# Emission by rank, lazily given operand buffers and one-buffer builders in a streaming encoder step

## Chip, core and metric

The kernel runs on one core of a Trainium2 chip. The metric is device time in microseconds of one execution; a kernel's time is the median of its runs.

## The reference, cut to what matters

Two layers run over 1024 prompt tokens and 32 sample tokens, 1056 in all. A layer normalises, projects, mixes with latent attention and retention, projects back and adds; then comes the part that the change touches:

```python
def channel_and_ple(h, p_i, norm_ffn_w, w_ff1, w_ff2, norm_ple_w, w_ple_gate, w_ple_proj):
    u = rms_norm(h, norm_ffn_w) @ w_ff1
    h = h + jnp.square(jax.nn.relu(u)) @ w_ff2
    gate = jax.nn.sigmoid(rms_norm(h, norm_ple_w) @ w_ple_gate)
    return h + (p_i @ w_ple_proj) * gate
```

The model width is 1024, the feed-forward width 4096, the depth 2.

## The kernel before

Activations stand with features on partitions and the 1056 tokens along the free dimension. `h` (8 x 1056, f32) stays in SBUF for the whole run. Every f32 factor of a product is split into two f16 halves, `hi` by ACT (a copy) and `lo` by DVE or POOL (the f32 value less `hi`), and a product is three f16 matmuls.

**The feed-forward products** use a two by two block scheme with seven products in place of eight. A weight unit `W[n]` has seven combined weights, each split; an operand has seven forms too, numbered 0 to 6, and product i of 1 to 7 takes the form `PROD[i]`: 1 takes 0, 7 takes 5, 6 takes 4, 4 takes 2, 5 takes 3, 2 takes 1 and 3 takes 6, in this order of work. `PROD` and the token groups are constants: three thirds `PG` of 2 x 176 tokens and two halves `PW` of 2 x 264. There are 32 weight units in a layer: four rounds `e` with four units of ff1 and then four of ff2. The first two units of ff1 go third by third, both side by side; all later ones go in halves. A product on one half is a block of twelve matmuls (four operand tiles, three matmuls each).

**Entry.** The output projection runs third by third (lines 1787 to 1806). `norm_chain` (L631) follows it: squares on ACT, their sums on PE, a power on POOL, a diagonal on ACT, its broadcast on PE (`acc,ones` in PE's order), then four times `four` (L717), which multiplies two tiles of `h` (DVE), makes four sums and differences, and splits the seven forms into the operand `x2`. `four` held one arena buffer `R` and one temporary `R3`.

**ff1 and ff2.** `ff1_units` (L943) runs the seven products of its units; product partial sums are read out of PSUM after each product and go on being added to in the same bank (`A` collects 1, 6, 5 and 3). `ff1_chains` (L870) evacuates (`ra`, `rb`), applies the squared relu and builds the seven forms of the ff2 operand `rr`; the pair of forms (4, 5) was split by one instruction on both (`r<-ra,r`, 2 x 264). `ff2_units` (L965) multiplies `rr` and adds into `h`.

**Buffers.** `arena` has 29 large SBUF buffers, `temps` 12 smaller ones, `weights` 14, `stages` 2 for incoming weights; PSUM has eight banks of four kinds (`mm`, `mx`, `st`, `o`). `operands` (L768) took all buffers of two operands at once, and the caller waited until seven were free.

**What sets the order.** The program text is not the order. `Pipe` (L300) holds generators in a heap and `Model` keeps an estimated time for each engine. A chain yields an operation, `_step` emits it when the model says that its inputs and its engine are ready; PE's instructions are written by the main thread, which polls the heap between blocks. `Either` (L202) picks between DVE and POOL for a two-input operation: before, by the earlier start with a bias of 0.2 us for the first named. What is emitted first stands first in its engine's queue, and every queue runs in order. `load_group` (L801) combines the weights of a unit with four subtractions and splits seven weights, `load` (L1027) starts it.

## Time and profile before

| | |
|---|---|
| runs (3) | 2709.64, 2712.25, 2714.51 us; median 2712.25 |
| the profiled execution | 2710.96 us, its span 2709.2 us |
| mean granted clock of TensorE | 0.974 |
| TensorE (PE) busy | 2566.6 us, 95% of the span |
| VectorE (DVE) busy | 1866.6 us, 69% |
| ScalarE (ACT) busy | 1310.0 us, 48% |
| GpSimd (POOL) busy | 1056.2 us, 39% |
| bytes moved | 130.53 MB, mean 48 GB/s |

In the rows of the profile L285 is the line that records every operation of DVE, ACT and POOL and L476 the one of all matmuls, so a row is told apart by its tiles: `out<-in`, shape, count. `ra<-st` is the copy out of a PSUM bank of kind `st`. In brackets stands the idle time before an instruction, and which instruction ended it.

### The profile page before, as it was taken

How to read it: one execution, taken by the hardware profiler on the slowest of the kernel's cores; microseconds unless marked ns; L12 is line 12 of the kernel's file. 1: busy time of each engine (PE TensorE's matmuls, PEld its weight loads, DVE VectorE, ACT ScalarE, POOL GpSimd, SP SyncE). 2: the span in 40 equal slices, each digit the busy share in tenths (PEclk: the TensorE clock that was granted, in tenths of full speed). 3: DMA queues.
4: the chain of work that ended last, by engine and by line, in shares of the span. 5: the costliest groups of instructions: out<-in, count | busy, mean ns of one | idle time of the engine just before them, and what ended most of it. 6: DMA issues, size and time to landing. Idle time of an engine off the chain costs nothing.

```text
span 2709.2 us, 58534 instructions
## 1 busy us (share of the span) xinstructions
PE 2566.6 (95%) x23322; PEld 2006.0 (74%) x23322; DVE 1866.6 (69%) x4555; ACT 1310.0 (48%) x3277; POOL 1056.2 (39%) x1267
## 2 busy tenths in 40 slices
PE   7998989988999999999999989999799999999997
PEld 4765667768888888887656556777688888888965
DVE  6767776656667585875657677775585766768755
ACT  6533366646345262635445344665462534536342
POOL 7123355654333332433331334564732333333331
PEclk8999989989999999999999999999899999999999
DMA  4201010000111212121112011100011111122112
GB/s 136 71 28 49 17 53 27 21 9 33 51 60 52 67 40 75 43 68 50 56 53 70 9 41 34 58 6 29 13 40 50 57 52 59 53 66 68 56 44 64
DMA packets 87057, 130.53 MB, mean 48 GB/s; under 512 B 11584, under 2 KB 36448, under 8 KB 86784
## 3 DMA queue, kind: packets, MB, share of 16 engines
q1 hardware_dynamic: 86496, 126.25, 15.1%
q8 instruction: 182, 2.98, 0.4%
q14 instruction: 91, 0.75, 0.1%
q10 hardware_dynamic: 288, 0.55, 0.1%
HBM read 116.98 MB, written 7.02 MB: 46 GB/s over the span
## 4 chain that ended last, share of the span: by engine, by line
PE 86%; DVE 8%; POOL 3%; ACT 2%; issue 1%; DMA 0%; DVEq 0%; POOLq 0%; ACTq 0%
PE mm L476 33%; PE o L476 20%; PE st L476 19%; PE mx L476 12%; DVE r L285 3%; POOL x L285 1%; PE st L483 1%; PE mx L483 1%; DVE ra L285 1%; DVE w L285 1%; POOL r L285 1%; DVE sf L285 0%; DVE mt L285 0%; PE mm L483 0%; DVE h L285 0%
## 5 line engine op out<-in xcount | busy, mean ns | idle before, releaser
L476 PEld LDWEIGHTS <-w 128*128 128x128 f16 x13176 | 1276.5, 99 | 315.6 <-issue 50.3
L476 PE MATMUL mm<-w,x 128*128 128x256 f16 (+3 forms) x1920 | 334.9, 326 | 11.6 <-DVE sil L285 6.0
L476 PEld LDWEIGHTS <-x 128*128 128x128 f16 x2304 | 222.0, 99 | 147.7 <-DVE sil L285 10.8
L476 PE MATMUL st<-x,w 128*128 128x264 f16 (+2 forms) x1896 | 247.0, 284 | 19.1 <-ACT ra L285 19.1
L285 DVE SCALAR_TENSOR_TENSOR w<-s,w 128x512 f16<-128x512 f32 (+2 forms) x280 | 216.5, 779 | 16.5 <-ACT w L285 14.9
L476 PE MATMUL mm<-x,w 128*128 128x264 f16 (+2 forms) x1800 | 224.7, 281 | 1.3 <-DVE rb L285 1.3
L285 ACT ACTIVATE w<-t 128x512 f16<-128x512 f32 x186 | 111.0, 623 | 226.3 <-POOL t L285 224.9
L476 PE MATMUL o<-x,w 128*128 128x264 f16 (+1 forms) x1608 | 209.7, 282 | 0.0
L476 PE MATMUL mm<-r,w 128*128 128x264 f16 (+1 forms) x1584 | 189.0, 275 | 20.6 <-DVE r L285 20.6
L285 POOL TENSOR_TENSOR pp<-e,pp 128x512 f16<-128x512 f32 (+1 forms) x160 | 169.9, 1073 | 73.9 <-ACT pp L285 59.4
L476 PE MATMUL o<-r,w 128*128 128x264 f16 (+1 forms) x1584 | 196.4, 275 | 0.0
L285 POOL TENSOR_TENSOR t<-stage,s 128x512 f32<-128x512 f32 x64 | 83.8, 1310 | 279.7 <-DMA stage<-in_wts_dram 242.8
L476 PE MATMUL st<-r,w 128*128 128x264 f16 (+1 forms) x1512 | 187.7, 276 | 0.5 <-DVE r L285 0.5
L285 ACT ACTIVATE w<-s 128x512 f16<-128x512 f32 (+2 forms) x280 | 166.8, 599 | 38.3 <-DMA s<-in_wts_dram 23.6
L285 POOL TENSOR_TENSOR t<-s,t 128x512 f32<-128x512 f32 x64 | 81.6, 1275 | 264.5 <-DVE w L285 234.8
L285 ACT ACTIVATE w<-stage 128x512 f16<-128x512 f32 (+1 forms) x130 | 79.3, 613 | 175.7 <-POOL stage L285 159.0
L285 DVE SCALAR_TENSOR_TENSOR w<-t,w 128x512 f16<-128x512 f32 x186 | 135.0, 734 | 26.6 <-ACT w L285 25.4
L285 DVE SCALAR_TENSOR_TENSOR h<-mm,h 128x264 f32<-128x264 f32 (+4 forms) x184 | 82.7, 449 | 88.2 <-PE mm L476 87.4
L285 POOL TENSOR_TENSOR r<-r 128x176 f32<-128x176 f32 (+2 forms) x94 | 67.6, 729 | 154.9 <-ACT qh L285 73.0
L285 DVE SCALAR_TENSOR_TENSOR h<-o,h 128x264 f32<-128x264 f32 (+2 forms) x150 | 64.1, 429 | 91.6 <-PE o L476 90.6
L476 PE MATMUL mx<-x,w 128*128 128x264 f16 (+2 forms) x984 | 124.4, 282 | 0.8 <-DVE w L285 0.8
L476 PE MATMUL st<-qh,k 97*128 97x256 f16 (+5 forms) x672 | 123.7, 259 | 0.0
(293 smaller groups left out, 5049.6 us busy)
## 6 DMA issues: line engine op xcount, KB each, us to landing
s<-in_wts_dram SPq DMA_DIRECT2D x256, 256.0 KB
stage<-in_wts_dram SPq DMA_DIRECT2D x64, 512.0 KB
out_dram<-r SPq DMA_DIRECT2D x24, 176.0 KB
s<-in_wts_dram SPq DMA_DIRECT2D x20, 192.0 KB
h<-in_xT_dram SPq DMA_DIRECT2D x6, 512.0 KB
s<-in_wts_dram SPq DMA_DIRECT2D x16, 144.0 KB
k<-kr SPq DMA_DIRECT2D x16, 136.1 KB
out_dram<-cn SPq DMA_DIRECT2D x16, 128.0 KB
```

The source lines that it names most:

```text
L285: x = f(*args, **kw)
L476: keep(nc.tensor.matmul(out, lhsT, rhs, start=start, stop=stop, skip_group_check=skip))
L483: keep(nc.tensor.transpose(out, in_, ident))
```

## The change

It has six parts.

1. `Pipe` gets a rank. Chains that are due at the same model time are emitted in order of rank, then of arrival. Norm chains have the rank of their third plus one, the ff1 chains 2 to 4 by form, weights and the rest 5; a chain's children inherit its rank.
2. `Either` compares the modelled ends of the two choices, and emits at the start of the chosen one.
3. `four` does with one arena buffer: `s2` and `s4` overwrite parts of `R`; the pair (4, 6) is split one by one. The norm's sums and diagonal use temporaries in place of an arena buffer.
4. In `ff1_chains` form 5 is made and split as soon as `y21` is there, ahead of form 4, each by an instruction of its own.
5. `operands` gives no buffers any more; `room_for` gives them as the products come to need them.
6. `load(2)` waits until form 0 of all thirds is there; a weight unit's transfers start when an arena buffer and both staging buffers are free; `weight` takes an open half buffer first; the projections poll.

```diff
@@ class Op, Either
+    def end(self):
+        ins, outs, n = self.engine.parts(self.args, self.kw)
+        return self.when() + self.engine.cost(self.name, ins, outs, n)
...
+    def choice(self):
+        a, b = self.ops
+        return a if a.end() <= b.end() + self.bias else b
+
     def when(self):
-        return min(op.when() for op in self.ops)
+        return self.choice().when()
 
     def emit(self):
-        a, b = self.ops
-        (a if a.when() <= b.when() + self.bias else b).emit()
+        self.choice().emit()
@@ class Pipe
-    def push(self, t, gen, op):
-        heapq.heappush(self.q, (t, self.n, gen, op))
+        self.rank = 5
+
+    def push(self, t, gen, op, rank=None):
+        heapq.heappush(self.q, (t, self.rank if rank is None else rank, self.n, gen, op))
@@ def weight
-        if weights.free:
+        if weights.free and not half:
@@ def norm_chain / four
-        def four(k, R, R3):
+        def four(k, R):
...
-            s2, s4 = R3[:, :w], R3[:, w:2 * w]
+            s2, s4 = y21, s1
...
-            yield tt(pool, s4, y12, s2, op=ALU.subtract)
-            pipe.spawn(split((4, 6), halves(R3[:, :n]), a, w, dve))
-            pipe.spawn(split((1, 2), halves(R2[:, :n]), a, w, pool))
-            yield lambda: parts[0] == 0
-            drop(R, R3)
+            pipe.spawn(split((4,), s2, a, w, dve))
+            pipe.spawn(split((1, 2), halves(R2[:, :n]), a, w, pool))
+            yield lambda: 3 in parts
+            yield tt(pool, s4, y12, s2, op=ALU.subtract)
+            pipe.spawn(split((6,), s4, a, w, dve))
+            yield lambda: len(parts) == 7
+            drop(R)
...
-                yield lambda: room(1 if g == 0 else 6) and arena.free
-                pipe.spawn(four(k, slot("r", (P, 2, HALF), F32), T("r")))
+                yield lambda: arena.free
+                pipe.spawn(four(k, slot("r", (P, 2, HALF), F32)))
@@ def operands
+    def room_for(op, *pairs):
+        for pr in pairs:
+            if pr[0] in op["o"]:
+                continue
+            if len(pr) == 2 or not op["shared"]:
+                pipe.wait(lambda: arena.free)
+                op["t"].append(slot(f"op{pr[0]}"))
...
@@ def ff1_chains
+            def s3():
+                yield from split_ops(op, (5,), lo, a, w, dve)
+                u.got.add("x5")
+
             def c11():
                 pipe.spawn(y11())
+                yield u.has("y21")
+                yield dve.q.tensor_tensor(lo, u.f, up, op=ALU.subtract)
+                pipe.spawn(s3())
                 yield u.has("s1")
-                yield dve.q.tensor_tensor(up, u.f, up, op=ALU.subtract)
-                yield dve.q.tensor_tensor(lo, s1, u.f, op=ALU.subtract)
+                yield dve.q.tensor_tensor(up, s1, u.f, op=ALU.subtract)
                 u.got.add("s2")
-                yield from split_ops(op, (4, 5), halves(Ra[:, :2 * w]), a, w, dve)
-                yield u.has("s4")
+                yield from split_ops(op, (4,), up, a, w, dve)
+                yield u.has("s4", "x5")
                 drop(Ra)
-            pipe.spawn(c11())
+            pipe.spawn(c11(), rank=2)
@@ def ff1_units
                 u.prod(i, name, kind, start)
+                room_for(u.op, *{5: ((2, 3),), 2: ((0, 1), (4, 5)), 3: ((6,),)}.get(i, ()))
@@ def load
                 def wait():
-                    yield lambda: n in staged
+                    yield lambda: n in staged and (cond is None or cond())
@@ main
-            pipe.spawn(norm_chain(g, vb + V_FFN, x2done, ops=x2, fin=fin, hold=slot("acc", (P, 2, HALF), F32)))
+            pipe.spawn(norm_chain(g, vb + V_FFN, x2done, ops=x2, fin=fin, hold=True), rank=g + 1)
...
-                        load(2)
+                        load(2, lambda x2=x2: all(len(x["n"][0]) == 6 for x in x2))
```

The lines of code that this moves can't be read from the diff, so here are three places of the orders before and after.

**PE at the entry of the first layer.** `acc,ones` with 128 columns is the broadcast of the third norm; `ma` are the output projection's operands, `x` and `op` the feed-forward's. Before:

```order
L476 LDWEIGHTS w
L476 MATMUL o<-ma_8447,w 128x352
L476 MATMUL mx<-ones,acc 128x1 x2
L476 MATMUL mx<-ones,acc 96x1
L476 MATMUL o<-acc,ones 128x128 x2
L476 MATMUL o<-acc,ones 128x96
L476 LDWEIGHTS w
L476 MATMUL st<-x_8764,w 128x176
```

After, where the projection ends:

```order
L490 LDWEIGHTS w
L490 MATMUL mm<-ma_8468,w 128x352
L490 LDWEIGHTS w
L490 MATMUL mm<-ma_8468,w 128x352
L490 LDWEIGHTS w
L490 MATMUL o<-op_8772,w 128x176
```

and ten blocks of twelve matmuls later:

```order
L490 LDWEIGHTS we
L490 MATMUL st<-op_8782,we 128x176
L490 MATMUL st<-acc_9150,ones 128x128 x2
L490 MATMUL st<-acc_9150,ones 128x96
L490 LDWEIGHTS w
L490 MATMUL mx<-op_8773,w 128x176
```

The broadcast stood ahead of the first product and now stands behind the tenth block.

**ACT at the same place.** `x<-r` and `op<-r` are the `hi` copies of the builder's forms, `ra<-st` and `ra<-o` read a product's partial sum out of PSUM. Before:

```order
L285 ACTIVATE x_8772<-r 128x2x176
L285 ACTIVATE x_8773<-r 128x2x176
L285 ACTIVATE x_8776<-r 128x2x176
L285 ACTIVATE x_8777<-r 128x2x176
L285 ACTIVATE ra<-st 128x176
L285 ACTIVATE ra<-o 128x176
L285 ACTIVATE rb<-mm 128x176 x2
L285 ACTIVATE w<-s 128x512
```

After, with the last splits of the last third and the first copies of the second third's products:

```order
L292 ACTIVATE op_8780<-r 128x2x176
L292 ACTIVATE op_8779<-r 128x2x176
L292 ACTIVATE op_8781<-r 128x176
L292 ACTIVATE op_8774<-r 128x176
L292 ACTIVATE op_8785<-r 128x176
L292 ACTIVATE w<-s 128x512
L292 ACTIVATE o<-o 128x176 x2
L292 ACTIVATE op_9583<-o 128x176
L292 ACTIVATE st<-st 128x176
L292 ACTIVATE ra<-o 128x176
L292 ACTIVATE ra<-st 128x176
```

The first third's `ra` copies stood behind all splits of the last third; now the second third's stand there.

**DVE at the first passage from ff1 to ff2**, with buffer numbers: `op4` and `r14` hold the pair (4, 5), `ra_10466` and `ra_10500` belong to the second half of the tokens. Before:

```order
L285 TENSOR_TENSOR ra_10466<-mx_10676,ra_10466 128x264
L285 TENSOR_TENSOR ra_10466<-rb_10467,mx_10676 128x264
L285 SCALAR_TENSOR_TENSOR h_88<-st_10755,h_88 128x264
L285 TENSOR_TENSOR r_10463<-o_10493,ra_10466 128x264
L285 TENSOR_TENSOR r10_10193<-st_10468,r10_10193 128x264
L285 TENSOR_TENSOR r10_10193<-o_10493,r10_10193 128x264
L285 SCALAR_TENSOR_TENSOR h_88<-mm_10775,h_88 128x264
L285 SCALAR_TENSOR_TENSOR w_10738<-s_10647,w_10738 128x512
L285 SCALAR_TENSOR_TENSOR w_10797<-stage_10649,w_10797 128x512
L285 SCALAR_TENSOR_TENSOR w_10800<-t2_10737,w_10800 128x512
L285 TENSOR_TENSOR r12_10194<-rb_10467,r12_10194 128x264
L285 TENSOR_TENSOR r14_10195<-ra_10466,r14_10195 128x2x264
```

After:

```order
L292 TENSOR_TENSOR ra_10498<-rb_10499,mx_10696 128x264
L292 TENSOR_TENSOR op0_10711<-mx_10696,op0_10711 128x264
L292 TENSOR_TENSOR ra_10500<-mx_10716,ra_10500 128x264
L292 TENSOR_TENSOR op0_10711<-mx_10716,op0_10711 128x264
L292 TENSOR_TENSOR op4_10712<-ra_10498,op4_10712 128x264 x2
L292 TENSOR_TENSOR rb_10501<-ra_10500,mm_10568 128x264
L292 TENSOR_TENSOR op2_10668<-mm_10568,op2_10668 128x264
L292 SCALAR_TENSOR_TENSOR h_88<-st_10772,h_88 128x264
L292 TENSOR_TENSOR op0_10711<-o_10502,op0_10711 128x264
L292 TENSOR_TENSOR op4_10712<-ra_10500,op4_10712 128x264
L292 TENSOR_TENSOR ra_10500<-rb_10501,mx_10716 128x264
L292 SCALAR_TENSOR_TENSOR h_88<-o_10797,h_88 128x264
```

The split of form 5 of the second half (the third row from the end) stands ahead of that half's form 4, where both were split by one instruction near the end.

## Rows read from the trace of the kernel before

**Rows 1.** The page, engines: busy us, share of the span, instructions.

```profile
PE 2566.6 (95%) x23322; PEld 2006.0 (74%) x23322; DVE 1866.6 (69%) x4555; ACT 1310.0 (48%) x3277; POOL 1056.2 (39%) x1267
```

**Rows 2.** Windows: stretch, its us, busy PE, PEld, DVE, ACT, POOL; PEclk, DMA, GB/s.

```profile
592.00:656.00 64.00, 44.76 (x519) 44.21 (x520) 43.94 (x113) 35.35 (x109) 39.70 (x48) 0.81 0.05 18
656.00:1262.00 606.00, 595.53 (x5296) 514.27 (x5295) 422.53 (x864) 273.72 (x642) 201.59 (x173) 0.99 0.18 56
1920.00:1984.00 64.00, 44.97 (x501) 44.24 (x500) 42.46 (x109) 34.59 (x106) 37.77 (x48) 0.81 0.06 18
1984.00:2590.00 606.00, 594.78 (x5294) 514.16 (x5292) 427.40 (x868) 272.76 (x642) 203.06 (x174) 0.99 0.18 56
```

**Rows 3.** Waits of PE, 592 to 656: us in total, times, longest.

```profile
PE st L476 <- ACT ra L285: 9.5, 1, 9.5
PE o L476 <- ACT acc L285: 7.7, 1, 7.7
```

**Rows 4.** Timeline of PE, 590 to 660: start, us, instruction, matmuls [idle before].

```profile
591.38 0.61 PE L476 MATMUL o<-ma,w 128*128 128x352 f16 x3
603.09 1.97 PE L476 MATMUL st<-x,w 128*128 128x176 f16 x12
618.61 1.92 PE L476 MATMUL st<-x,w 128*128 128x176 f16 x12 [9.47 <-ACT ra L285]
654.77 1.07 PE L476 MATMUL o<-x,we 128*128 128x176 f16 x12
655.68 1.51 PE L476 MATMUL o<-x,w 128*128 128x264 f16 x12
```

**Rows 5.** Timeline of DVE, POOL and ACT, 600 to 620.

```profile
603.34 4.02 DVE L285 SCALAR_TENSOR_TENSOR r<-h,vec,o 128x352 f32<-128x352 f32 x8 [3.63 <-PE o L476]
608.19 5.10 POOL L285 TENSOR_TENSOR r<-r 128x176 f32<-128x176 f32 x5 [2.38 <-DVE r L285]
618.26 0.30 ACT L285 ACTIVATE ra<-st 128x176 f32<-128x176 f32 x1
```

**Rows 6.** Waits of PE, 656 to 1262, then 1984 to 2590.

```profile
PE mm L476 <- DVE r L285: 9.9, 4, 3.5
PE mm L476 <- DVE r L285: 10.7, 4, 3.5
```

**Rows 7.** Timeline of DVE and PE at the first passage to ff2.

```profile
700.94 1.76 DVE L285 TENSOR_TENSOR r<-ra,r 128x528 f16<-128x528 f32 x1
702.76 0.39 PE L476 MATMUL mm<-r,w 128*128 128x264 f16 x2 [3.50 <-DVE r L285]
702.98 2.52 PE L476 MATMUL o<-r,w 128*128 128x264 f16 x12
705.29 2.22 PE L476 MATMUL st<-r,w 128*128 128x264 f16 x12
711.40 1.51 PE L476 MATMUL st<-r,w 128*128 128x264 f16 x12
```

**Rows 8.** Instruction groups by form: busy us, mean ns | idle before, releaser.

```profile
L285 POOL TENSOR_TENSOR x<-r,x 128x352 f16<-128x352 f32 x103 | 93.4, 926 | 22.3 <-ACT x L285 22.2
L285 POOL TENSOR_TENSOR r<-r 128x176 f32<-128x176 f32 x58 | 38.6, 681 | 28.6 <-DVE r L285 20.9 <-issue 7.6
L285 DVE TENSOR_TENSOR x<-r,x 128x352 f16<-128x352 f32 x41 | 31.0, 772 | 8.5 <-ACT x L285 8.5
L285 DVE TENSOR_TENSOR x<-r,x 128x176 f16<-128x176 f32 x20 | 9.8, 514 | 0.0
L285 DVE TENSOR_TENSOR r<-r 128x176 f32<-128x176 f32 x38 | 13.2, 399 | 0.0
L285 DVE TENSOR_TENSOR r<-ra,r 128x528 f16<-128x528 f32 x50 | 53.7, 1083 | 0.4 <-ACT r L285 0.4
L285 DVE TENSOR_TENSOR r<-mm,r 128x264 f16<-128x264 f32 x56 | 23.7, 424 | 3.5 <-ACT r L285 3.5
L285 DVE SCALAR_TENSOR_TENSOR w<-t,w 128x512 f16<-128x512 f32 x186 | 135.0, 734 | 26.6 <-ACT w L285 25.4
```

More of the change, by code (lines that the diff above doesn't have):

```diff
@@ L629, with norm_chain @@
     turn = [0, 0]
-    def norm_chain(g, wbase, done, xs=None, ops=None, final=None, fin=None, hold=None):
+    def norm_chain(g, wbase, done, xs=None, ops=None, final=None, fin=None, hold=False):
         a, w = PG[g]
@@ L639, in norm_chain @@
         hv = lambda k: halves(h[:, k])[:, :, a:a + w]
-        if hold is None:
-            yield lambda: room(3)
-            acc = [T("acc0"), T("acc1")]
-        else:
-            acc = [hold[:, 0], hold[:, 1]]
+        yield lambda: room(3)
+        acc = [T("acc0"), T("acc1")]
+        if hold:
             ps = yield from take("mx")
@@ L654, in squares @@
                 yield lambda: fin is None or k in fin
-                if hold is not None:
+                if hold:
                     yield act.q.activation(halves(ac[:, :n]), hv(k), AF.Square)
@@ L674, in norm_chain @@
         pool.memset(rs, 1.0)
-        if hold is None:
+        if not hold:
             yield Need(model, acc[0][:, :n], acc[1][:, :n])
@@ L680, in norm_chain @@
                     mm(ps[:tn, j:j + 1], acc[z][:, o:o + tn], ones[:, 0:1], start=z == 0, stop=z == 1)
-            drop(*acc)
+            drop(acc[1])
         lr = tl[-1][1]
@@ L687, in norm_chain @@
         yield pool.q.tensor_tensor(rs[:, 4:4 + nt], rs[:, :nt], pw[:, :nt], op=ALU.pow)
-        diag = (yield from gT("diag")) if hold is None else acc[0]
+        if hold:
+            drop(acc[1])
+        diag = acc[0]
         for j, (o, tn) in enumerate(tl):
@@ L694, in norm_chain @@
             mm(pb[:, o:o + tn], ones[:tn, :], diag[:tn, o:o + tn], start=True, stop=True)
-        drop(diag if hold is None else hold)
+        drop(diag)
         rbv = halves(pb[:, :n])
@@ L765, with operands @@
     PAIRS_X = ((0, 5), (1, 2), (4, 6), (3,))
-    PAIRS_R = ((0, 1), (2, 3), (4, 5), (6,))
-    def operands(name, nk, pairs):
-        out, single = [], None
-        for k in range(nk):
-            op = {"t": [], "p": {}, "o": {}, "n": [set() for _ in range(7)]}
-            for pr in pairs:
-                if len(pr) == 2 or k % 2 == 0:
-                    op["t"].append(slot(f"{name}{k}{pr[0]}"))
-                    sl = op["t"][-1].rearrange("p a (o t) -> p a o t", o=2)
-                if len(pr) == 2:
-                    op["p"][pr] = sl
-                    op["o"][pr[0]], op["o"][pr[1]] = sl[:, :, 0], sl[:, :, 1]
-                else:
-                    single = sl if k % 2 == 0 else single
-                    op["o"][pr[0]] = single[:, :, k % 2]
-            out.append(op)
-        return out
+    def operands(nk):
+        out = [{"t": [], "p": {}, "o": {}, "n": [set() for _ in range(7)], "z": k % 2} for k in range(nk)]
+        for k in range(0, nk, 2):
+            out[k]["shared"] = out[k + 1]["shared"] = []
+        return out
+    def room_for(op, *pairs):
[5 more added lines that the diff above has]
+                op["t"].append(slot(f"op{pr[0]}"))
+                sl = op["t"][-1].rearrange("p a (o t) -> p a o t", o=2)
+            if len(pr) == 2:
+                op["p"][pr] = sl
+                op["o"][pr[0]], op["o"][pr[1]] = sl[:, :, 0], sl[:, :, 1]
+            else:
+                if not op["shared"]:
+                    op["shared"].append(sl)
+                op["o"][pr[0]] = op["shared"][0][:, :, op["z"]]
     def stage(layer, u):
@@ L1025, in plan, with load, wait @@
         staged = {}
-        def load(n):
+        def load(n, cond=None):
             def after():
+                def wait():
+                    yield lambda: arena.free and len(stages.free) == 2
+                    staged[n + 1] = stage(L, us[n + 1])
                 if n + 1 < len(us):
-                    staged[n + 1] = stage(L, us[n + 1])
+                    pipe.spawn(wait())
             if n < len(us):
                 def wait():
-                    yield lambda: n in staged
+                    yield lambda: n in staged and (cond is None or cond())
                     yield from load_group(W[n], staged[n], after)
@@ L1783 @@
         pipe.wait(lambda: len(arena.free) >= 18)
-        x2 = operands("x2", KT // 2, PAIRS_X)
+        x2 = operands(KT // 2)
+        for op in x2:
+            room_for(op, *PAIRS_X)
         x2done = set()
```

37 lines of the change are left out of this document (20 added, 17 removed).

## The prediction

> **What bounds the kernel now.** I read the engine table first: TensorE (PE) is busy 2566.6 of 2709.2 us [rows 1], so it idles 142.6 us, and no other engine is above 69%. The question for a change of order is where PE's idle time lies and what ends it. The table of windows gives that [rows 2]. In the 64 us at 592 to 656, where the first layer enters its feed-forward part, PE is busy 44.76 us and its granted clock is 0.81; the second layer's entry at 1920 to 1984 reads the same (44.97, 0.81). The 606 us behind each entry hold all other feed-forward chunks; there PE idles 606 - 595.53 = 10.5 us and 606 - 594.78 = 11.2 us. The four windows hold 60 of the 142.6 us.
>
> PE's waits name the releasers. At the entry it is ScalarE (ACT) twice: 9.5 us for `ra` and 7.7 us for `acc` [rows 3]. The timeline shows the place [rows 4]: the output projection's last matmuls start at 591.38, the first products of the feed-forward part at 603.09, the fifth block of them only at 618.61, and the first product of the third weight unit, 42 blocks of twelve matmuls after the start, at 655.68. A block takes 655.68 - 654.77 = 0.91 us there, so 42 need 38.2 us; from 592.0 the stretch takes 63.7. **25.5 us are lost per layer.** Why ACT is late stands in [rows 5]: the copy of `ra` out of PSUM is ready to go long before 618.26, but the ACT queue holds the operand splits of the last token third in front of it; these wait for GpSimd (POOL), which at 608.19 spends 5.10 us on five subtractions.
>
> In the 606 us stretches the wait is PE for VectorE (DVE) `r`: 9.9 and 10.7 us, four times each [rows 6], once per passage from a ff1 chunk to its ff2. One passage is in [rows 7]: DVE starts the pair split `r<-ra,r` at 700.94 and holds it 1.76 us, PE resumes at 702.76 after 3.50 us. Its next two blocks take 2.52 and 2.22 us where a block takes 1.51 eight us later: PE has fallen to the lower of its two clock levels (1.2 for 2.4 GHz), which costs 1.0 and 0.7 us.
>
> **The change part by part, entry.** Counted over the whole orders, the change moves work from POOL (300 instructions fewer) to DVE (409 more), because `Either` now compares ends, not starts; ACT gets 84 more because two pairs are split one by one. At the entry 83 of the 103 splits that POOL did (0.926 us each) leave it; on DVE the same form has cost 0.772, the half form 0.514 [rows 8]. The order of PE matters more. Before, the broadcast of the third norm stands ahead of the first product; behind the change it stands ten blocks later. PE therefore starts its products when the projection ends, at about 592 + 0.2, and runs ten blocks to about 601.5 without the 7.7 us wait.
>
> What is late next: the build of the third token third. It begins with the broadcast, 0.8 us, as before at 601.7, then eight multiplications on DVE in 4.02 us [rows 5], then by the order of DVE 13 subtractions (0.399), twelve half splits (0.514) and six whole ones (0.772) [rows 8]: 5.2 + 6.2 + 4.6 = 16.0. With five other steps of 0.42 that is 22 us by these means, which hold POOL's interference, or 18 by the shortest rows, so it ends at 619 to 624, hardly before it ended. In ACT's order the copy `ra` of the second third stands behind the last of those splits, and the products that add into that bank need it. So PE runs 14 blocks of the first third and four of the second, and stops at about 609 until ACT is through, some 2 us before the build's end: 617 to 619. From there 24 of the 42 blocks remain, 21.8 us, and one or two of them at the lower clock, 1 us: the third unit starts at 641 instead of 655.7. **14 us per layer, 28 in all.** Bounds: 5 us, if the build ends nine later (DVE is 43.94 of 64 us busy there and gets more); 23 us, if nothing of it is on PE's path.
>
> Weights: `load(2)` now waits for the first quarter of all groups. Its DVE splits follow the build in the order and its last ACT split stands before the third unit's first PSUM copy; seven pairs of splits at 0.734 [rows 8] are 5 us in a time of 22 in which PE has blocks. Nothing, unless the build slips; then it slips with it, and that is in the lower bound.
>
> **Passages to ff2.** In DVE's order the split that PE waits for, pair (4,5) of the second half, stood 23 instructions behind the evacuation `ra<-mx,ra` of that half; now the split of operand 5 alone stands 13 behind. Ten steps of 0.42 are 4.2 us, and it holds DVE 0.42 instead of 1.76. The longest of the eight waits is 3.5 us, so all should go: 9.9 + 10.7 = 20.6 us. The half-clock blocks behind them add 1.7 us each at perhaps four of the eight, some 6; I take 24 for both and bound it by 12 (half of the waits come back at operand 4 or 2) and 27.
>
> Cutting the pairs adds instructions. The row says that it costs nothing: the pair on DVE takes 1.083 us in the mean, two halves 0.85 [rows 8]. The Trainium skill (Perfetto Trace Analysis, Optimizing Scalar/DVE Operations) says the contrary for a saturated engine, since each instruction carries a fixed overhead of about 60 ns on DVE, and that fewer, larger operations raise throughput; 100 halves for 50 pairs would by that be 50 x 0.06 = 3 us of DVE work more, an estimate from its figure, and the sum would stay where it is, as DVE is not saturated behind the entry.
>
> **Weight combinations.** 152 of the 256 subtractions that combine weights go from POOL to DVE. DVE shows none of that form; the nearest row of that size with two inputs from SBUF, `w<-t,w`, has 0.734 [rows 8], the contended one, and I take it: 112 us of DVE in all, and 20 for 48 `r` splits, less 11 for the pairs, so 60 per layer. DVE's share of the 606 us goes from 422.5 to 483, 80%. The cover is PE's own time there; it holds on the average, and near the passages the planner leaves POOL as the other choice. ACT's 84 instructions lie beside PE too: ACT is busy 273.72 of 606 us and 35.35 of 64 [rows 2].
>
> **Everything else** (start, attention, gate, final norm; diag in a buffer at hand; polling inside the projections; the same 498 transfers on SP, some in other places): these stretches hold the other 83 us of PE's idle time, and other choices of engine move it a little either way. I take 0 and bound it by 6 us up or down.
>
> **Sum.** 28 + 24 + 0 = 52 us off the profiled execution's 2710.96 gives 2659. The median of the runs, 2712.25, lies 1.3 above that execution, so the forecast is **2660 us**. A measurement of this kernel can tell 0.2%, 5.4 us, from no change.
>
> **Rivals.**
> 1. *The entry keeps its length.* DVE and POOL may hinder each other so that the build ends 13 us later and PE stands at the same 655. For it: POOL's 5.10 us for five steps that otherwise take 0.681 [rows 5, 8], all while DVE ran. Against: POOL has little left to do there. Only the 24 us remain: 2711 - 24 + 1 = 2688. The Trainium skill (same page and section) supports it: the two engines share a read port of the SBUF, so that moving work between them might not help. The trace agrees in part: those five steps show it.
> 2. *The entry is free.* If the build runs ahead of the order's worst place, PE never stops: 2 x 23 + 25 = 71 us, 2641. For it: before, ACT was late because of POOL, not of DVE. Against: the copies behind the splits in ACT's queue.
> 3. *DVE becomes the bound, slower than before.* The place is the 606 us stretches. It decides where DVE's 483 us grow by 606/483 = 1.25. The contended pair stands at 1.083/0.848 = 1.28 of its two halves, so this is not absurd. At 1.3 DVE needs 628 us, 22 over, in both layers 44; the passages' gain is gone, the entry gives perhaps 14 instead of 28: 2711 + 44 - 14 + 1 = 2742. Against: the ratio came from POOL, which loses 300 instructions.
> 4. *The waits move on.* PE meets the next operand (4 at the passages, the second third at the entry) as late as the old one: within 5 us of 2712.
>
> **How the numbers follow.** Forecast 0.63, rival 1 0.12, rival 2 0.13, rival 3 0.07, rival 4 0.05. The forecast's own range: entries 2 x 9 to 2 x 19, passages 18 to 27, rest -3 to +3, so gains of 33 to 68 and 2644 to 2679. To leave out no more than two in ten it reaches to both neighbours, 2637 to 2691. Faster: 0.63 + 0.12 + 0.13 = 0.88; same 0.05; slower 0.07.
>
> **What would show it.** In the profile of the changed kernel: PE's first `op` product right behind the last `ma` product, near 592; one PE wait of 5 to 10 us for ACT `ra` near 609 in place of two; the clock of that 64 us window above 0.9; the third unit's first product near 641. In the 606 us stretches the eight waits for DVE gone, and PE busy within 3 us of the whole; DVE about 80%, POOL about 15% there. It is wrong if PE's wait for the build lasts beyond 15 us, if weights (`w`) release PE behind the entry, or if DVE's steps of one form grow instead of shrink.

## The result and the profile after

The changed kernel takes **2652.26 us** (median of four runs, 2650.53 to 2653.48), the kernel before 2711.86 on the same chip: a ratio of 0.9779, 95% interval 0.9762 to 0.9796, 60 us faster. The forecast was 2660, in a range of 2637 to 2691.

The engine line of the changed kernel's page answers to [rows 1]; in its rows L292 is the line of all DVE, ACT and POOL operations and L490 that of the matmuls.

```profile
PE 2554.6 (96%) x23322; PEld 2003.1 (76%) x23322; DVE 1982.7 (75%) x4964; ACT 1309.1 (49%) x3361; POOL 718.5 (27%) x967
```

PE idles 96.9 us of 2651.5 where it idled 142.6. 116 us of DVE work came in and 338 us of POOL work went. The windows that answer to [rows 2] show where PE gained (stretch, its us, busy PE, PEld, DVE, ACT, POOL; PEclk, DMA, GB/s):

```profile
592.00:656.00 64.00, 54.89 (x604) 52.84 (x603) 56.05 (x173) 41.28 (x139) 15.45 (x22) 0.89 0.12 38
656.00:1262.00 606.00, 606.00 (x5390) 521.96 (x5388) 485.60 (x1024) 285.06 (x691) 95.27 (x90) 1.00 0.19 60
1894.00:1958.00 64.00, 53.97 (x616) 52.17 (x614) 57.17 (x174) 41.59 (x138) 12.50 (x18) 0.92 0.12 38
1958.00:2564.00 606.00, 605.29 (x5363) 521.02 (x5362) 482.37 (x1020) 282.69 (x686) 95.49 (x91) 1.00 0.18 58
```

In the 606 us behind the first entry PE is busy for all of the 606, at the full clock, and the table of PE's waits has no row there; the second layer's stretch loses 0.7 us, in its last ff2 unit. All eight waits of [rows 6] are gone. DVE has 485.6 of 606 us, 80%, POOL 15.7%. The entries have a higher clock (0.89 and 0.92 for 0.81) and two shorter waits each. PE's waits from 592 to 656 (us in total, times, longest), in place of [rows 3]:

```profile
PE o L490 <- ACT ra L292: 4.7, 1, 4.7
PE st L490 <- DVE r L292: 4.4, 1, 4.4
```

PE's timeline in that window, in place of [rows 4] (start, us, instruction, matmuls, idle before in brackets):

```profile
595.19 0.85 PE L490 MATMUL o<-op,w 128*128 128x176 f16 x9
...
605.42 0.84 PE L490 MATMUL st<-acc,ones 128*128 128x128 f32 x6
...
615.25 1.94 PE L490 MATMUL st<-op,we 128*128 128x176 f16 x12 [4.44 <-DVE r L292]
...
618.75 1.86 PE L490 MATMUL mm<-op,we 128*128 128x176 f16 x12
625.27 1.92 PE L490 MATMUL o<-op,w 128*128 128x176 f16 x12 [4.67 <-ACT ra L292]
...
631.47 1.07 PE L490 MATMUL o<-op,w 128*128 128x176 f16 x12
...
649.68 1.51 PE L490 MATMUL st<-op,w 128*128 128x264 f16 x12
```

The first `op` product stands right behind the last `ma` product, as forecast. The broadcast (`acc,ones`) comes ten blocks later, at 605.42, into a bank of kind `st`. The first wait is for that bank: the second unit's first product on the second third needs it, and cannot have it until DVE has read the broadcast out. The second wait is for the copy `ra`. DVE and ACT show why both are late:

```profile
610.93 0.58 DVE L292 SCALAR_TENSOR_TENSOR r<-h,vec,st 128x352 f32<-128x352 f32 x1
...
611.67 3.52 DVE L292 SCALAR_TENSOR_TENSOR r<-h,vec,st 128x352 f32<-128x352 f32 x7
...
616.37 3.87 ACT L292 ACTIVATE op<-r 128x176 f16<-128x176 f32 x12
621.40 0.35 ACT L292 ACTIVATE op<-r 128x176 f16<-128x176 f32 x1 [1.16 <-DVE r L292]
623.03 0.35 ACT L292 ACTIVATE op<-r 128x176 f16<-128x176 f32 x1 [1.28 <-DVE r L292]
...
625.11 0.31 ACT L292 ACTIVATE ra<-st 128x176 f32<-128x176 f32 x1
```

DVE's queue holds ff1's steps in front of the eight multiplications that read the broadcast, so they begin 5.5 us after it and end at 615.2. ACT does twelve splits of the last third before the copies out of PSUM, and then two more, before each of which it stands idle for over a microsecond until DVE has made the input. Behind the first wait three blocks take 615.25 to 620.61, 5.4 us where 2.7 would do, and behind the second four take 625.27 to 631.47, 6.2 us where 3.6 would do: the lower clock level (a granted clock of 0.52 from 615.2 to 620.6).

For every kernel below I compare stages of the two layers. The entry runs from the end of the last `ma` product to the first product on 264 columns (595.4 to 649.68 above). "Halves" are all ff chunks from there to the first product on 176 columns of the last ff2 unit. Both come from the one profiled execution of each kernel.

| kernel | entry, us | halves, us | median, us |
|---|---|---|---|
| before | 63.7, 65.1 | 562.4, 564.2 | 2711.9 |
| changed | 54.3, 53.5 | 548.1, 548.1 | 2652.3 |
| either_alone | 57.9, 57.8 | 574.3, 574.2 | 2735.7 |
| ranks_alone | 64.6, 63.1 | 551.9, 555.1 | 2691.1 |
| no_either | 57.9, 58.9 | 549.9, 549.9 | 2663.6 |
| no_ranks | 54.4, 54.1 | 572.1, 571.9 | 2706.5 |
| pair45_again | 54.5, 53.9 | 550.2, 550.2 | 2654.9 |
| weights_last | 49.8, 48.6 | 555.3, 555.3 | 2658.2 |
| eager_buffers | 53.4, 52.2 | 552.6, 554.3 | 2658.0 |
| two_buffer_builders | 52.4, 53.6 | 552.5, 552.9 | 2658.8 |
| form6_later | 47.8, 47.5 | 556.6, 556.4 | 2654.7 |
| form6_later_w2 | 49.9, 50.3 | 555.0, 553.3 | 2653.8 |
| weights_to_pool | 50.6, 50.2 | 561.6, 560.0 | 2669.8 |
| form6_later_w34 | 48.5, 47.6 | 559.3, 558.7 | 2660.7 |

The change's 57.7 us of span (2709.2 - 2651.5) are so 21.0 at the entries, 30.5 in the halves, and 6.2 in all the rest. In the halves of the changed kernel PE has no idle time and the full clock throughout, so 548.1 us is what these products take there without a wait.

### The profile page after: what moved, and what is told of

Read it like the earlier page. It is cut to its first block, busy times and chain, and to the rows that moved or that the text cites. A ratio compares the mean times of both kernels' runs of the same rounds, so it can differ in the third digit from the quotient of the medians.

```text
span 2651.5 us, 58580 instructions
## 1 busy us (share of the span) xinstructions
PE 2554.6 (96%) x23322; PEld 2003.1 (76%) x23322; DVE 1982.7 (75%) x4964; ACT 1309.1 (49%) x3361; POOL 718.5 (27%) x967
## 4 chain that ended last, share of the span: by engine, by line
PE 90%; DVE 6%; ACT 1%; DMA 1%; issue 1%; POOL 0%; DVEq 0%; POOLq 0%; SPq 0%; ACTq 0%
PE mm L490 35%; PE st L490 21%; PE o L490 20%; PE mx L490 13%; DVE r L292 1%; PE mx L497 1%; PE st L497 1%; DVE w L292 1%; DMA s<-in_wts_dram 1%; DVE op L292 1%; DVE mt L292 0%; PE mm L497 0%; ACT w L292 0%; DVE sf L292 0%; DVE y L292 0%
## 5 line engine op out<-in xcount | busy, mean ns | idle before, releaser
L490 PEld LDWEIGHTS <-w 128*128 128x128 f16 x13176 | 1270.8, 98 | 274.4 <-issue 16.1
L490 PE MATMUL o<-op,w 128*128 128x264 f16 (+1 forms) x3072 | 376.8, 274 | 10.3 <-ACT ra L292 10.3
L490 PE MATMUL st<-op,w 128*128 128x264 f16 (+1 forms) x2928 | 362.7, 275 | 0.3 <-DVE h L292 0.3
L490 PE MATMUL mm<-op,w 128*128 128x264 f16 (+1 forms) x3072 | 361.4, 275 | 0.0
L490 PE MATMUL mm<-w,x 128*128 128x512 f16 (+3 forms) x1944 | 337.5, 325 | 9.2 <-DVE sil L292 5.4
L490 PEld LDWEIGHTS <-x 128*128 128x128 f16 x2304 | 222.4, 99 | 143.6 <-issue 8.3
L292 ACT ACTIVATE w<-stage 128x512 f16<-128x512 f32 (+1 forms) x130 | 79.2, 613 | 255.9 <-DVE stage L292 241.6
L292 DVE SCALAR_TENSOR_TENSOR w<-s,w 128x512 f16<-128x512 f32 (+2 forms) x280 | 191.4, 689 | 12.7 <-ACT w L292 11.2
L292 POOL TENSOR_TENSOR pp<-e,pp 128x512 f16<-128x512 f32 (+1 forms) x160 | 173.8, 1097 | 79.3 <-ACT pp L292 61.5
L490 PE MATMUL mx<-op,w 128*128 128x264 f16 (+1 forms) x1608 | 186.1, 272 | 0.0
L292 ACT ACTIVATE w<-s 128x512 f16<-128x512 f32 (+2 forms) x280 | 166.9, 600 | 21.3 <-DMA s<-in_wts_dram 14.2
L292 POOL TENSOR_TENSOR op<-rb,op 128x264 f16<-128x264 f32 (+1 forms) x38 | 27.2, 715 | 526.6 <-ACT op L292 342.2
L292 POOL TENSOR_TENSOR t<-stage,t 128x512 f32<-128x512 f32 x40 | 53.3, 1332 | 391.6 <-DVE t L292 379.5
L292 ACT ACTIVATE w<-t 128x512 f16<-128x512 f32 x186 | 110.6, 621 | 79.0 <-DVE t L292 38.7
L292 DVE SCALAR_TENSOR_TENSOR w<-t,w 128x512 f16<-128x512 f32 x186 | 128.9, 693 | 15.5 <-ACT w L292 15.3
L292 DVE SCALAR_TENSOR_TENSOR h<-mm,h 128x264 f32<-128x264 f32 (+4 forms) x187 | 84.2, 450 | 57.6 <-PE mm L490 55.8
L490 PE MATMUL st<-qh,k 97*128 97x256 f16 (+5 forms) x672 | 123.3, 262 | 0.3 <-ACT e L292 0.2
L292 ACT ACTIVATE e<-st 128x512 f32<-128x512 f32 (+1 forms) x192 | 90.8, 489 | 61.4 <-PE st L490 55.2
L292 DVE SCALAR_TENSOR_TENSOR h<-st,h 128x264 f32<-128x264 f32 (+2 forms) x152 | 65.0, 430 | 62.5 <-PE st L490 59.6
L292 DVE TENSOR_REDUCE mt<-mx 128x1 f32<-128x512 f32 (+4 forms) x194 | 102.5, 540 | 11.2 <-PE mx L490 9.5
L490 PEld LDWEIGHTS <-k 96*128 96x128 f16 (+3 forms) x1008 | 86.8, 99 | 20.4 <-issue 3.6
L490 PE MATMUL mm<-mr,w 128*128 128x384 f16 (+1 forms) x576 | 99.5, 316 | 0.1
```

The lines of the kernel that those rows point to most:

```text
L292: x = f(*args, **kw)
L490: keep(nc.tensor.matmul(out, lhsT, rhs, start=start, stop=stop, skip_group_check=skip))
```

## The experiments

### One part at a time, at the passages

**either_alone**: before, with part 2 of the change.

```diff
+    def choice(self):
+        a, b = self.ops
+        return a if a.end() <= b.end() + self.bias else b
     def when(self):
-        return min(op.when() for op in self.ops)
+        return self.choice().when()
```

> The kernel before with one part of the change alone: Either compares modelled ends. In PE's order this alone puts the broadcast of the third norm behind the first six blocks of products instead of ahead of the first. Theory A (the entry is gained by the order of PE's queue and by a build that POOL no longer delays, the passages by form 5 that is split first): the two entries shrink by about 10 us each, the eight waits for the pair split in the 606 us stretches stay (about 10 us per layer), so about 2692 us. Theory B (one part does it all: POOL's work moves to DVE, and what delayed both places was POOL): entries and passages shrink, about 2660. Theory C (Either matters only together with the lazily given buffers): 2712 within 5.

Measured: 2735.7 us, ratio 1.0087 (1.0068 to 1.0106), **slower than before**. No theory had this. The entries gain 6 to 7 us each, but each ff stretch in halves is 10 to 12 us longer: PE waits 4.4 us at each of its four passages, with some 2 us of lower clock behind each wait. These two stages make 9 of the 28 us by which this profile is longer than that of the kernel before. The other 19 lie outside them, 9 before the first entry and 11 between the first layer's feed-forward part and the second entry (less 0.3 at the end); the start alone can differ by 4.5 without a change, as the last section shows. Between the layers PE's waits for `k` and `v` come to 7.5 us, where they were 1.5. No run looks further into these 19 us. DVE's timeline at one passage:

```profile
859.81 1.18 DVE L292 TENSOR_TENSOR r<-ra,r 128x528 f16<-128x528 f32 x1
860.92 0.68 DVE L292 SCALAR_TENSOR_TENSOR w<-s,w 128x512 f16<-128x512 f32 x1
861.52 0.68 DVE L292 SCALAR_TENSOR_TENSOR w<-stage,w 128x512 f16<-128x512 f32 x1
862.12 0.68 DVE L292 SCALAR_TENSOR_TENSOR w<-t,w 128x512 f16<-128x512 f32 x1
862.73 0.69 DVE L292 TENSOR_TENSOR r<-ra,r 128x528 f16<-128x528 f32 x1
```

and what PE does meanwhile:

```profile
863.47 2.45 PE L483 MATMUL mm<-r,w 128*128 128x264 f16 x14 [4.43 <-DVE r L292]
```

Three splits of weights (`w`), 0.68 us each, stand in DVE's queue between the two pair splits. PE's product needs the second pair, the weights are for a later unit. They hold DVE for 1.8 of the 4.4 us; the two pair splits have another 1.9.

**no_either**: the change without part 2.

```diff
-        return a if a.end() <= b.end() + self.bias else b
+        return a if a.when() <= b.when() + self.bias else b
```

> The changed kernel, but Either compares starts as before. POOL gets its operand splits and weight combinations back. Theory A: the passages stay free of waits, since form 5 is still first, and the entries give back half of their 21 us: 2662 to 2668 us. Theory B (Either does it all): most of the 60 us is lost, 2700 or more. Theory C: all the same as the changed kernel, 2652.

Measured: 2663.6 (ratio 0.9819, 0.9801 to 0.9836), Theory A's number. No passage has a wait (the halves are 1.8 us longer, 1.6 of it one wait for a weight), the entries give back 3.6 and 5.4 us.

**pair45_again**: the change without part 4.

```diff
+                yield u.has("s1")
                 yield dve.q.tensor_tensor(lo, u.f, up, op=ALU.subtract)
-                pipe.spawn(s3())
-                yield u.has("s1")
                 yield dve.q.tensor_tensor(up, s1, u.f, op=ALU.subtract)
-                yield from split_ops(op, (4,), up, a, w, dve)
+                yield from split_ops(op, (4, 5), halves(Ra[:, :2 * w]), a, w, dve)
```

(`lo` and `up` have changed places there, so that the pair lies in order.)

> The changed kernel, but the forms 5 and 4 are again split by one instruction, after both are made. Theory A: the eight waits of PE for DVE at the passages come back with the half clock behind them, 20 to 31 us, so 2672 to 2683, and the entries stay as they are. Theory B (the rank or the lazily given buffers shortened the queue in front of the split): the waits stay away, 2652 within 5.

Measured: 2654.9 (0.9789, 0.9771 to 0.9808); the waits stay away. Theory A falls: it was not form 5's early split that freed the passages. In the stretch in halves of each layer PE waits once, 1.9 us for `w`, and the stretch is 2.1 us longer. A pair split of 1.67 us is on DVE again, and PE's 24 matmuls that begin beside it show no wait:

```profile
848.22 1.67 DVE L292 TENSOR_TENSOR op<-ra,op 128x528 f16<-128x528 f32 x1
...
848.31 2.86 PE L490 MATMUL mm<-op,w 128*128 128x264 f16 x24
```

**no_ranks**: the change without part 1.

```diff
-        heapq.heappush(self.q, (t, self.rank if rank is None else rank, self.n, gen, op))
+        heapq.heappush(self.q, (t, 5, self.n, gen, op))
```

> The changed kernel, but every chain has the same rank, so that only the time and the order of arrival count. In PE's order the broadcast of the third norm then stands behind 5.75 blocks of products, not ten. Theory A (ranks are a small part): the entries give back up to 5 us each, the passages nothing: 2652 to 2662. Theory D (the ranks keep DVE's and ACT's queues short at both places): passages and entries both give back, 2680 or more.

Measured: 2706.5 (0.9982, 0.9972 to 0.9991): nearly all of the gain is gone, Theory D. The entries stay at 54; the halves rise by 24.0 and 23.8 us. Waits of PE in the first (650 to 1222):

```profile
PE o L490 <- DVE op L292: 15.4, 4, 3.8
PE mm L490 <- DVE op L292: 1.1, 4, 0.3
```

DVE and PE at the second passage:

```profile
852.53 1.16 DVE L292 SCALAR_TENSOR_TENSOR w<-s,w 128x512 f16<-128x512 f32 x1
...
854.30 0.68 DVE L292 SCALAR_TENSOR_TENSOR w<-stage,w 128x512 f16<-128x512 f32 x1
854.90 0.68 DVE L292 SCALAR_TENSOR_TENSOR w<-t,w 128x512 f16<-128x512 f32 x1
855.50 0.42 DVE L292 TENSOR_TENSOR op<-ra,op 128x264 f16<-128x264 f32 x1
...
855.97 0.60 PE L490 MATMUL o<-op,w 128*128 128x264 f16 x2 [3.84 <-DVE op L292]
```

Form 5 is early here, and PE waits for form 4 (`op<-ra,op` at 855.50), behind three weight splits of 1.16, 0.68 and 0.68 us. The same place in the changed kernel has no weight instruction on DVE from 833.8 to 846.0, and PE runs through:

```profile
839.13 1.26 DVE L292 TENSOR_TENSOR op<-ra,op 128x264 f16<-128x264 f32 x2
...
841.38 2.86 PE L490 MATMUL mm<-op,w 128*128 128x264 f16 x24
```

The waits at the four passages are 15.4 + 1.1 = 16.5 of the 24.0 us; the other 7.5 are the lower clock behind them, 1.9 at each.

**ranks_alone**: before, with part 1 and nothing else.

```diff
-            pipe.spawn(c11())
+            pipe.spawn(c11(), rank=2)
-            pipe.spawn(c12())
+            pipe.spawn(c12(), rank=4)
```

(and so for the other chains, with the heap's key of part 1.)

> The kernel before with the ranks alone (norm chains, ff1 chains, weights last), nothing else of the change. Without ranks the changed kernel's two ff stretches in halves took 572.1 and 571.9 us, with them 549.0, and the entries took 54 us in both. Theory D (ranks shorten the queue in front of the operand splits at the passages, alone): the stretches go from 563.4 and 565.1 to about 550, the entries stay at 64, so about 2683. Theory E (ranks matter only where Either has put the weight combinations on DVE; before, they were on POOL): the passages keep their waits of 2 to 3 us, 2712 less 5 at the most.

Measured: 2691.1 (0.9937, 0.9917 to 0.9957). Theory E falls, Theory D holds with a smaller sum: the halves shrink by 10.5 and 9.1 us, the entries stay at 64.6 and 63.1. Where the weight combinations stand on POOL, ranks gain 10 us a layer; where `Either` has put them on DVE, 24.

**weights_last**: the change, all builders of one rank, weights behind them.

```diff
-            pipe.spawn(c21(), rank=3)
+            pipe.spawn(c21(), rank=2)
-            pipe.spawn(c12(), rank=4)
+            pipe.spawn(c12(), rank=2)
```

(c22 and both norm chains of the ff part get 2 as well.)

> The changed kernel, with one rank for all builders (norm and ff1 chains 2) and 5 for the weights as before: weights last, but no order among the builders. Theory D1 (what stood in front of the late split was weight work): the passages stay free, 2652 within 5. Theory D2 (the order of the forms among themselves does it): the waits for op come back, 23 us per layer, about 2695.

Measured: 2658.2 (0.9805, 0.979 to 0.9819). PE waits for no `op` in the halves: in the changed kernel **weights behind all builders is enough to free the passages** (D1); the order among the builders isn't needed. The time missed D1's bound by a microsecond: PE now waits 4.7 us for `w` in the halves, of which the next part has more.

### The entry

**eager_buffers**: the change without part 5.

```diff
+                    pipe.wait(lambda: len(arena.free) >= 7)
                     rr += operands(2)
+                    for op in rr[-2:]:
+                        room_for(op, (0, 1), (2, 3), (4, 5), (6,))
```

> The changed kernel, with the operand buffers of two units taken at once, after a wait until seven are free, as before. The broadcast of the third norm then stands behind 3.5 blocks in PE's order instead of ten. Theory F (the lazily given buffers make the entry shorter by letting PE run ahead): each entry gives back about 5 us, 2662. Theory G (the entry ends where the third build and ACT's copies behind it end, whatever PE ran first): the waits only change places, 2652 within 3.

Measured: 2658.0 (0.9805, 0.979 to 0.982). The entries are no longer, but 1 us shorter, as G has it: in place of waits of 4.4 and 4.7 there are one of 1.3 for `ra` and one of 8.2 for the broadcast's bank. But the halves are 4.5 and 6.3 us longer, with a wait of 3.0 and 3.8 us for `w`, so the time misses G's bound by 3 us.

**two_buffer_builders**: the change with the builder of before.

```diff
-                pipe.spawn(four(k, slot("r", (P, 2, HALF), F32)))
+                pipe.spawn(four(k, slot("r", (P, 2, HALF), F32), T("r")))
```

(`four` is the one of before, with `R3`, one split for forms 4 and 6, and the condition in front of it.)

> The changed kernel, with the builder of the entry as before: a temporary for forms 4 and 6, both split by one instruction. Either alone made the entries 57.9 us (63.7 before), the whole change 54.3, and neither the ranks nor the lazily given buffers account for the rest (54.4 and 53.4 without them). Theory P (the one-buffer builder, which starts its splits one by one, gives the rest): entries of about 58, so about 2659. Theory G (the builder's form does not matter): 2652 within 4.

Measured: 2658.8 (0.981, 0.9795 to 0.9825). The time is P's, the reason is not: the entries are 52.4 and 53.6, no longer than with one buffer, and the halves are 4.4 and 4.8 us longer, with a wait of 2.96 us for `w`.

**form6_later**: the change, but the chain that splits form 6 asks for its buffer.

```diff
-                room_for(u.op, *{5: ((2, 3),), 2: ((0, 1), (4, 5)), 3: ((6,),)}.get(i, ()))
+                room_for(u.op, *{5: ((2, 3),), 2: ((0, 1), (4, 5))}.get(i, ()))
...
                 u.got.add("s4")
+                yield lambda: 6 in op["o"] or op["shared"] or arena.free
+                room_for(op, (6,))
```

> The changed kernel, but the buffer of form 6 is asked for by the chain that splits it and no longer by the thread that writes PE's and ACT's queues. That thread stood still there at both entries until a builder of the last token third gave its buffer back, and so ACT's copies of the second third's partial sums stand behind the operand splits of the last third. In this kernel they stand between them. Theory H (ACT's order makes the wait for ra of 4.7 and 5.6 us): that wait goes, and with the half clock behind it each entry is 4 to 7 us shorter, 2638 to 2645. Theory G (the build of the last third ends the entry in any order): the wait comes back for op or r, 2652 within 3.

Measured: 2654.7 (0.9795, 0.9781 to 0.981). H is right of the place: the wait for `ra` is gone and the entries are 6.5 and 6.0 us shorter. ACT's copy of the second third, 625.11 in the changed kernel, with the entry starting 3 us earlier:

```profile
614.02 0.32 ACT L292 ACTIVATE ra<-st 128x176 f32<-128x176 f32 x1 [0.39 <-PE st L490]
```

But the halves are 8.5 and 8.3 us longer, and the time is G's. PE's waits from 592 to 1197:

```profile
PE mm L490 <- DVE w L292: 4.8, 2, 3.0
PE st L490 <- DVE r L292: 4.7, 1, 4.7
PE st L490 <- DVE w L292: 1.2, 1, 1.2
PE mm L490 <- DVE rb L292: 1.2, 1, 1.2
```

The longest wait for `w`, on DVE's and PE's timelines:

```profile
686.91 0.69 DVE L292 SCALAR_TENSOR_TENSOR w<-stage,w 128x512 f16<-128x512 f32 x1
```
```profile
687.65 4.32 PE L490 MATMUL mm<-op,w 128*128 128x264 f16 x22 [2.96 <-DVE w L292]
```

The split of the fifth unit's product 7, `w<-stage,w`, stands behind builder steps that fill DVE without a gap. The changed kernel's entry and halves come to 602.4 and 601.6 us, this one's to 604.4 and 603.8, those of weights_last, eager_buffers and two_buffer_builders to 604 to 607. What an entry gains there comes back as waits for weights within the next 50 us.

**form6_later_w2**: that kernel, and without the condition of part 6.

```diff
-                        load(2, lambda x2=x2: all(len(x["n"][0]) == 6 for x in x2))
+                        load(2)
```

> The kernel with form 6's buffer asked for later, and load(2) without its condition. In that kernel each entry was 6 us shorter (47.8 and 47.5 us for 54.3 and 53.5), and the stretch in halves behind it 7.5 us longer (556.6 and 556.4 for 549.0), with PE waiting for w of the third and fourth unit. Theory W1 (those weights are late because load(2) starts only when all first forms are built): the waits for w go, the stretches return to 549 to 551, about 2640. Theory W2 (they are late because DVE, busy 46 of 50 us there, takes them last, or because their buffers come free only as PE uses up the units before): nothing changes, 2652 to 2656.

Measured: 2653.8 (0.9787, 0.9771 to 0.9803). W1 falls: the sum is 604.9 and 603.7, and waits of 1.9 and 3.0 us for `w` are there as before. The other pieces of part 6 were not tested by themselves.

**weights_to_pool**: form6_later, with the combinations biased to POOL.

```diff
-            yield tt(pool, t1, b12, b11, op=ALU.subtract)
+            yield tt(pool, t1, b12, b11, op=ALU.subtract, bias=1.0)
```

(and so the other three.)

> The kernel with form 6's buffer asked for later, and the weight combinations given to POOL again unless it would end over 1.0 us later than DVE (0.2 before): 362 of POOL's instructions work on 512 columns, 205 in the kernel it is made from. Theory W3 (the weights behind the entry are late because DVE is the busiest engine there): DVE is relieved, the waits for w go, both entries keep their 6 us: 2638 to 2645. Theory X (POOL beside DVE slows DVE's splits, as with the kernel before): entries of 55 us and more, and waits at the passages, 2655 to 2670.

Measured: 2669.8 (0.9848, 0.9833 to 0.9863). W3's number falls, but its reason is not tested. DVE is relieved from 700 to 800 (63.9 us busy, 75.8 in form6_later), where PE waits for no weights, and hardly where the waits are: it is busy 84.5 of the 98 us from 597 to 695, and 87.0 of the 98 from 592 to 690 in form6_later. The waits for `w` come to 4.2 us in the first layer, 6.0 there. The sum is 612.2 and 610.2, since a builder step (`rb`) now makes PE wait 1.0 us twice in each of the last three rounds. The time is in Theory X's range, without its longer entries.

**form6_later_w34**: form6_later, with two weight groups no longer last.

```diff
-                pipe.spawn(wait())
+                pipe.spawn(wait(), rank=2 if n in (3, 4) else None)
```

> The kernel with form 6's buffer asked for later, and the weight groups of the fourth and fifth unit (n = 3 and 4) with rank 2 instead of 5, so that they are no longer last. In every kernel with ranks so far, entry and stretch in halves together took 603 to 606 us (54.3 + 549.0, 47.8 + 556.6, 49.8 + 556.2, 53.4 + 552.6, 52.6 + 552.5): what the entry gained came back as waits for w at the third and fourth unit behind it. In DVE's order the split that PE waits for longest (fifth unit, product 7) moves 15 instructions forward. Theory R (the weights stand last by rank in a DVE queue that is full there): the waits for w go, the stretches return to 549 to 551, the entries stay at 48, about 2640 to 2645. Theory S (the weights' buffers come free only as PE works, so the sum is fixed by the chain of weights whatever DVE's order): the sum stays at 603 to 606, 2650 to 2655.

Measured: 2660.7 (0.9822, 0.98 to 0.9844). PE's waits for `w` shrink to 1.0 and 0.3 us, but it now waits 2.7 for `op` and 2.7 for `rb`: the sum rises to 607.8 and 606.3. So S's number came near and R's did not; S's reason is not shown. From 595 to 700 the changed kernel's DVE is busy 94.8 of 105 us, so a step that is moved forward there moves another back. Whether DVE alone fixes the sum of 602 stays open: weights_to_pool took most of its work from DVE behind these waits. No kernel here is faster than the changed one.

## Why the prediction held, and where its reasons failed

Three terms missed: over both layers the entries gave 7 us less than forecast, the passages 6.5 and the rest 6.2 more. That the sum came within 8 us is in part luck.

**The entry, 14 us per layer (9.4 and 11.6 measured).** The place and the order were right: first product at the projection's end, no 7.7 us wait, ACT's copy behind the splits. Two waits stand where one was forecast. The step that failed in the order is "runs 14 blocks of the first third and four of the second, and stops at about 609": PE stopped after 15 blocks, at 610.8, for a resource that the working had left out, the PSUM bank in which the broadcast still stood. That wait was 4.4 us, and the one for `ra` then 4.7 instead of 8 to 10, so both together, 9.1 us (10.0 in the second layer), came to what the one was to cost. The term that was mis-sized is "one or two of them at the lower clock, 1 us": it measured 5.2 us, six blocks behind the two waits, and 3.2 in the second layer, four blocks. The norm's small matmuls between the first blocks, 1.8 us, were not in the sum at all.

The wait for `ra` does not come from ACT's order alone: form6_later shows that this order came from a thread that stood still for an arena buffer. Of the parts, `Either` gives 6 to 7 us an entry alone, and without it the rest gives 6; without the ranks, without the lazily given buffers or with the old builder the entries are about as long or a little shorter.

**The passages, 24 us (30.5).** "Form 5 is split 13 instructions behind the evacuation instead of 23, so all waits go": they went, but not for that step. With form 5 first and no ranks they were longer than before (no_ranks); with the pair and ranks they were gone (pair45_again). I had read the shorter distance as a property of the new code in `ff1_chains`; the gain came with the ranks. Nor is the distance the measure: the 23 is that of the first passage, and at the other three it was 18. In ranks_alone the last pair split stands 18 behind there as well, and PE waits 0.6 to 1.6 us instead of 1.6 to 2.6. At the second passage its two pairs are split at 848.89 and 854.38, both by DVE; before, POOL split one at 854.76 and DVE the other at 855.04. Weight instructions are only a part of what ranks move. In either_alone three and in no_ranks four of them stand between evacuation and split, but in the kernel before three do so at the first passage of a layer and none at the other three. What cost the wait there is not shown by itself. The term for the lower clock was too small: the stretches were 14.3 and 16.1 us longer than the 548.1 they now take, the waits 20.6, which leaves 9.9, 1.2 at each of eight, where the working had 1.7 at four. And its own two parts, 20.6 and some 6, are more than the 24 that it took.

**The weight combinations, at nothing.** Right for the sum of busy time (80% of 606 forecast, 80.1% measured; 0.69 to 0.71 us for three of the four combinations and 1.33 for the fourth, for the assumed 0.734), wrong in what it said of cover: "PE's own time there" covers them only because ranks put them behind the operand splits. Without ranks the stretches in halves are 24 us longer (no_ranks), and `Either` put into the kernel before makes them 10 to 12 us longer (either_alone).

**The rest, 0 (6.2).** Just outside its bound of 6: the start up to the first entry is 3.4 us longer than before, the part between the layers 5.5 and the end 4.0 shorter. No run separates these, and the last section shows that the start can differ by 4.5 us without any change in it.

**The rivals.** Rival 3, slower by DVE, was priced 2742, and either_alone comes near it with 2735.7, but not by its mechanism, a longer duration of each step that fills DVE: DVE is busy 72% of that kernel's span, the stretches in halves lose 22 us for the rival's 44, through waits in which weight splits stand in DVE's queue, and 19 us are lost outside the stretches that the rival named. Rival 4 is what happened inside the experiments: form6_later turns a wait for `ra` into one for `w`. Rival 1's "13 us later" and rival 2's free entry did not come.

**What would show it.** As forecast: the eight waits gone, PE within 3 us of the 606 (606.00, 605.29), DVE 80%, POOL 15%. Not as forecast: one wait of 5 to 10 us (two of 4 to 6), the clock above 0.9 (0.89, then 0.92), the third unit 49 us behind the projection's end (54.3 and 53.5).

## To carry over

When a change gives one engine more work, ask of each place where another engine waits for it which instructions of other chains will stand in front, not only how busy it is: three weight splits of 0.68 us that nobody needed yet were 1.8 us of a wait of 4.4, on an engine that was 80% busy or less. Sort what nobody waits for behind what somebody waits for, and test each part alone: a part that pays only together with another can look harmful (`Either`), and a part that looks like the cause can be worth 2 us a layer (form 5 first). Before a wait is removed, look for the next one within the following 50 us; in seven kernels here the sum of the two stages stayed at 602 to 607 us while the entry moved by 7 and the halves by 8.

## What the runs showed of the hardware

**Two engines on one form.** A subtraction of two SBUF tiles of 512 columns takes DVE 0.69 us; where POOL runs a like one beside it, it mostly takes over twice that. Groups by form of the changed kernel (busy us, mean ns, idle before), and on the timeline one such pair and one subtraction with nothing of POOL beside it:

```profile
L292 DVE TENSOR_TENSOR stage<-stage 128x512 f32<-128x512 f32 x33 | 43.7, 1325 | 0.3
...
L292 DVE TENSOR_TENSOR t<-stage,s 128x512 f32<-128x512 f32 x33 | 22.8, 690 | 0.0
...
727.19 1.30 POOL L292 TENSOR_TENSOR t<-stage,t 128x512 f32<-128x512 f32 x1 [17.63 <-DVE t L292]
727.37 1.67 DVE L292 TENSOR_TENSOR stage<-stage 128x512 f32<-128x512 f32 x1
...
764.95 0.69 DVE L292 TENSOR_TENSOR stage<-stage 128x512 f32<-128x512 f32 x1
```

The mean of 1325 ns mixes two kinds. Of the 33 `stage<-stage`, the nine that no POOL instruction overlaps take 0.69 us; of the 24 beside a POOL `t<-stage,t`, 22 take 1.63 to 1.67 and two take 0.69, which stays open. DVE's 1.67 us above end 0.55 after POOL's 1.30. The Trainium skill (GPSIMD Engine Reference, Specifications) says that GpSimd's SBUF interfaces contend with DVE instructions that have two SBUF inputs; the trace agrees in 22 of the 24 cases, with 1.63 to 1.67 us for 0.69.

**The first 50 us are not the same twice.** The changed kernel and pair45_again have the same instructions up to the first entry. The same product starts 4.5 us later in the second profile:

```profile
24.41 0.61 PE L490 MATMUL mx<-ones,sq 128*128 128x1 f32 x4 [1.70 <-DVE sq L292]
...
75.68 1.51 PE L490 MATMUL o<-w,x 128*128 128x288 f16 x11 [0.20 <-DVE w L292]
...
0.00:50.00 50.00, 33.24 (x199) 22.00 (x200) 38.66 (x128) 31.03 (x96) 24.98 (x52) 0.86 0.50 163
```

and in pair45_again:

```profile
24.39 1.01 PE L490 MATMUL mx<-ones,sq 128*128 128x1 f32 x4 [1.70 <-DVE sq L292]
...
80.22 1.51 PE L490 MATMUL o<-w,x 128*128 128x288 f16 x11 [0.20 <-DVE w L292]
...
0.00:50.00 50.00, 37.84 (x190) 24.07 (x190) 35.06 (x115) 28.49 (x86) 21.80 (x43) 0.76 0.50 161
```

At 24.4 both engines are level, but the four small matmuls take 0.61 us in one and 1.01 in the other, and the granted clock of the first 50 us is 0.86 and 0.76. So a difference of a few microseconds between two spans says nothing of a change that lies behind them; stages tell more. They aren't exact either: entry and halves of both layers take 1204.0 us in the changed kernel and 1208.8 in pair45_again, 4.8 apart, and the medians are 2.6 apart.
